# Hybrid attention and retention layer: the last block of the projections in another order, its weights' room handed on group by group

## The chip, the cores and the metric

The kernel runs on one core of a Trainium2 chip. The metric is the device time of one execution in microseconds (us), and less is better. "Before" and "after" are the kernel without and with the change.

## What is computed

```python
h = rms_norm(x, norm_gain)                       # x: 4096 tokens x 1024
qa, ka, va, ga, qr, kr, vr, gr = split(h @ w_in)
attn = dilated_attention(rope(qa), rope(ka), va) # 8 heads x 64, three (window, dilation) branches
ret  = retention(rotate(qr), rotate(kr), vr)     # 4 heads, key 64, value 128, chunks of 128 tokens
ret  = group_norm(ret) * ret_gn_gain
out  = rms_norm(x + concat(silu(ga) * attn, silu(gr) * ret) @ w_out, final_gain)
```

All of it is float32. A float32 operand is held as a rounded part (hi) and a rest (lo), and a product is three matmuls (`mm3`, lines 49 to 51 of the profile): hi by hi, hi by lo, lo by hi.

## The kernel before

There are three phases. **Phase 1** projects blocks of 512 tokens (`BLK`, 8 blocks) onto q, k, the retention's q and k together (group r), and the attention's values v. A block has six half groups, `GROUPS`: q0, q1, k0, k1, r0, r1, each of two product tiles of 24 matmuls, and then four value tiles of 24 matmuls each. `rotate` (VectorE, lines 227 to 232, with ScalarE's `hl` for q and k at line 244) applies the positions' tables (`tabA` for q and k, `tabR` for r) and stores the result to device memory (`dr_q`, `dr_k`, `dr_r`) from SyncE's queue. It is called for a group when the next group's products have been issued. `store_values` (lines 257 to 266) scales a value tile on ScalarE into one of two tiles `vo` and issues six DMAs `dr_v<-vo` from ScalarE's queue: two of 256 KB, four of 64 KB.

**Phase 2** is the attention, head by head, from `dr_k` (a tile `kk` of 128 x 4096 for two heads) and `dr_q` (tiles q00 and q10 for the first half of the tokens, q01 and q11 for the second). S is the scores' matmul (line 615), P the exponentials on ScalarE. TensorE's gaps are filled with the retention by chunks of 128 tokens: V (the chunk's values, 24 matmuls of `w2` by `hc`), Rs (its scores) and so on, from a generator `filler`. Its order is set by a table of costs in nanoseconds: `LEAD` worth of it goes ahead of the first S, then a slot's worth behind each step of the attention. `hr` is a chunk of the transposed x (512 KB), `hc` its hi and lo halves (ScalarE line 404, GpSimdE line 405), `vch` the V tile copied out by ScalarE (line 984). **Phase 3** computes the gates and the output projection.

Every engine's order is fixed: the code is written in the order in which each engine issues it, and SyncE's and ScalarE's queues issue their DMAs in that order.

On the change of phase: the weights of q, k and r lie in a stack of pools. Behind the last block's groups (q, k, r) that stack is closed as a whole (`right.close(3)`, line 338), and the room goes to q, w2, the chunk tiles and kk. Everything of phase 2 is then loaded on SyncE's queue in the order `hr` (chunk 0), `w2` (8 DMAs of 256 KB), `kk` (4 of 512 KB), q00 and q10 (4 of 256 KB each), `hr` (chunk 1); `w2` is split into hi and lo, the last rotate is called, and the last block's four value tiles follow.

Each DMA of SyncE's and ScalarE's queues raises one of eight semaphores (DMAHW0 to DMAHW7), which are handed out in turn over both queues; a DMA that gets a semaphore waits at its issue until the DMA that had it before has landed, whichever queue that was on. A wait at the head of a queue holds everything behind it.

Of the kernel before, what the change touches and what calls it, by code (L numbers as in the profile page):

```python
# [8 lines left out]
F32 = mybir.dt.float32  # L9
# [8 lines left out]
LEAD = 1500.0  # L18
# [35 lines left out]
class Split:  # L54
# [3 lines left out]
    def __init__(self, nc, pool, name, src, ks=range(KT), scale=None):  # L58
        self.nc, self.pool, self.name, self.scale = nc, pool, name, scale
        self.src = [src[k * 128 : (k + 1) * 128, :] for k in ks]  # L60
        self.n, self.width = len(ks), src.shape[1]
        self.hi = pool.tile([128, self.n, self.width], F32R, name=f"{name}hi")
        self.raw, self.lo = {}, {}

    def slot(self, j, dtype):
        return self.pool.tile([128, self.width], dtype, tag=f"{self.name}{j}", name=f"{self.name}{j}")
# [6 lines left out]
    def split(self, j, lo_engine=None):  # L73
        hi, raw = self.hi[:, j, :], self.raw.pop(j)
# [12 lines left out]
    def at(self, j, cols):  # L87
        return self.hi[:, j, cols], self.lo[j][:, cols]
# [23 lines left out]
def phase1(tc, io, dr, right, ahead):  # L112
# [5 lines left out]
    with ExitStack() as ctx:  # L118
# [19 lines left out]
        W = {}  # L138
        for g in ("r", "k", "q", "v"):
            p = wp if g == "v" else right.open(f"p1w{g}")  # L140
            i = "qkrv".index(g)
            W[g] = Split(nc, p, f"w1{g}", io["w1"][:, i * 512 : (i + 1) * 512], scale=qgain if g == "q" else gain)
# [154 lines left out]

        GROUPS = [("q", 0), ("q", 1), ("k", 0), ("k", 1), ("r", 0), ("r", 1)]
        for b in range(NBLK):
            last = b + 1 == NBLK  # L300
            if b:
                tabA = load_tables(b, "A")
            xts, hnext, waiting = [], [], []
            for gi, (g, half) in enumerate(GROUPS):
# [8 lines left out]
                if gi == (0 if b else 2):  # L313
                    rb = along_free(b, diag)
                    scaled(tabA, rb)
                    if b:
                        tabR = load_tables(b, "R")
                        scaled(tabR, rb)
                waiting.append((g, half, ps))

                while len(waiting) > 1 and rb is not None:
                    w, x, (A, B) = waiting.pop(0)
                    rotate(b, w, x, A, B, tabR if w == "r" else tabA)
# [7 lines left out]
                if not last and gi >= 3:  # L331
                    while len(xts) < (2, 3, 4)[gi - 3]:
                        xts.append(load_xt(b + 1, len(xts)))
                    if gi == 4:
                        hnext.append(make_h(b + 1, 0, xts[0]))
            if last:
                right.close(3)
                qp = right.open("p2q")
                w2 = Split(nc, right.open("p2w2"), "w2", io["w2"], scale=gain)
                hcp = right.open("p2h")  # L340
                kka = right.open("p2ka")
                raw = load_x_chunk(nc, hcp, io, 0)
                ahead.update(w2=w2, qp=qp, hcp=hcp, kka=kka, hch={0: [split_h_chunk(nc, hcp, raw, 0, i) for i in range(2)]})
# [1040 lines left out]
```

## Time and profile before

| what | us |
|---|---|
| device time, median of three runs (2444.05, 2447.39, 2448.32) | 2447.39 |
| the profiled execution: its own time | 2448.65 |
| the profiled execution: span of the page | 2446.9 |
| TensorE matmul busy | 2343.5 (96%) |
| VectorE, ScalarE, GpSimdE busy | 1485.2, 989.6, 714.3 |

The page cuts the span into 40 slices of 61.2 us; its PE line is the busy share of TensorE in tenths, its PEclk line the clock that TensorE was granted, in tenths of full speed. The timeline lists instructions of one engine with their start and duration, and in brackets how long the engine had stood idle and what released it. The chain of waits is followed back from the last instruction to what released each step. A matmul's row is longer than the distance to the next, since they are pipelined: the distance of starts is what it costs.

### The profile page before, as it was taken

The numbers are of one execution on the slowest core, as the hardware profiler recorded it, in microseconds if no ns is written. First come the engines' busy times: TensorE is split into PE (matmuls) and PEld (weight loads), VectorE is DVE, ScalarE is ACT, GpSimd is POOL, SyncE is SP. The second block draws the span as 40 slices with busy tenths as digits, with TensorE's granted clock in tenths as the row PEclk, the third lists the DMA queues.
The fourth block names the chain that finished last, engine by engine and source line by source line (L and its number), as shares of the span: only waits on it lengthen the run. The fifth ranks groups of instructions, "written<-read, shape, count | busy, mean of one in ns | idle before, by whom it ended". The sixth has DMA issues, their size and how long they took to land.

```text
span 2446.9 us, 41800 instructions
## 1 busy us (share of the span) xinstructions
PE 2343.5 (96%) x14568; PEld 1985.9 (81%) x14568; DVE 1485.2 (61%) x3921; ACT 989.6 (40%) x2868; POOL 714.3 (29%) x761
## 2 busy tenths in 40 slices
PE   7999999999995999999999999996899999999998
PEld 5778888888884888887888887885889889999997
DVE  5643443444342878787777879786665565565554
ACT  4322212212212666666666666666222232232221
POOL 5312112112102535343444435354312112121110
PEclk9999999999997999999999999998999999999999
DMA  6343344343348565758576665746675656676663
GB/s 189 129 148 120 124 139 132 113 137 129 120 146 208 138 163 137 178 130 190 132 165 153 154 158 127 169 118 197 149 162 153 146 158 154 150 156 165 141 158 91
DMA packets 404067, 362.59 MB, mean 148 GB/s; under 512 B 191784, under 2 KB 334760, under 8 KB 398736
## 3 DMA queue, kind: packets, MB, share of 16 engines
q1 hardware_dynamic: 389216, 332.91, 52.5%
q10 hardware_dynamic: 14112, 25.43, 3.3%
q8 instruction: 115, 1.88, 0.3%
q0 software_dynamic: 528, 1.58, 0.2%
q14 instruction: 96, 0.79, 0.1%
HBM read 241.18 MB, written 118.64 MB: 147 GB/s over the span
## 4 chain that ended last, share of the span: by engine, by line
PE 74%; DMA 10%; DVE 5%; issue 2%; ACT 2%; POOL 2%; SPq 1%; ACTq 0%; POOLq 0%; DVEq 0%
PE S L615 8%; PE mm L49 8%; PE mm L50 8%; PE mm L51 8%; PE O L685 6%; PE T L652 5%; PE po L49 3%; PE po L50 3%; PE po L51 3%; PE g L50 3%; PE g L49 3%; PE g L51 3%; PE V L49 3%; DMA wb<-dr_w 2%; PE V L51 2%; PE V L50 2%
## 5 line engine op out<-in xcount | busy, mean ns | idle before, releaser
L636 DVE CUSTOM_DVE_ANT_0 S<-S,mask 128x256 f32<-128x256 f32 (+1 forms) x768 | 308.5, 402 | 168.7 <-PE S L615 139.1
L643 ACT ACTIVATE P<-S,nm 128x256 f32<-128x256 f32 (+1 forms) x768 | 337.4, 449 | 74.4 <-DVE nm L636 51.2
L51 PE MATMUL g<-h,wg 128*128 128x256 f32 x1024 | 290.6, 284 | 0.0
L652 PE MATMUL T<-ident,P 128*128 128x128 f32 x1368 | 213.3, 273 | 0.4 <-ACT P L643 0.4
L615 PE MATMUL S<-kk,qc 128*128 128x256 f32 x1024 | 186.5, 306 | 17.1 <-ACT P L643 11.8
L50 PE MATMUL po<-wo,m 128*128 128x512 f32 x512 | 201.7, 394 | 0.0
L51 PEld LDWEIGHTS g<-h,wg 128*128 128x128 f32 x1024 | 197.6, 193 | 0.1
L685 PE MATMUL O<-pt,v 128*64 128x128 f32 (+1 forms) x1968 | 196.0, 325 | 0.2 <-ACT pt L662 0.2
L615 PEld LDWEIGHTS S<-kk,qc 128*128 128x128 f32 x1024 | 149.8, 190 | 45.5 <-issue 28.9
L41 ACT ACTIVATE m<-e 128x256 fp32r<-128x256 f32 x128 | 53.3, 417 | 323.9 <-DVE e L1123 171.7
L405 POOL TENSOR_TENSOR hc<-hr,hc 128x512 fp32r<-128x512 f32 x64 | 85.9, 1343 | 319.3 <-ACT hc L404 249.4
L49 PE MATMUL po<-wohi,m 128*128 128x512 f32 x448 | 175.7, 392 | 2.1 <-DVE x L1170 2.1
L1177 POOL TENSOR_TENSOR rs<-v,mhalf 128x1 f32<-128x1 f32 x32 | 17.3, 541 | 549.2 <-DVE v L1175 549.2
L51 PE MATMUL po<-wohi,m 128*128 128x512 f32 x448 | 176.4, 394 | 0.0
L159 POOL TENSOR_TENSOR sq<-sq,sq 128x512 f32<-128x512 f32 x56 | 76.2, 1361 | 326.8 <-ACT sq L155 326.8
L685 PEld LDWEIGHTS O<-pt,v 128*64 128x64 f32 x1968 | 121.4, 136 | 60.7 <-issue 31.0
L652 PEld LDWEIGHTS T<-ident,P 128*128 128x128 f32 x1368 | 163.7, 141 | 1.1 <-ACT P L643 1.1
L49 PE MATMUL g<-h,wg1hi 128*128 128x256 f32 x512 | 146.5, 287 | 14.2 <-ACT h L439 14.2
L643 ACT ACTIVATION_READ_ACCUMULATOR P<-S,nm 128x1 f32 x768 | 158.0, 206 | 0.0
L50 PE MATMUL g<-h,wg1hi 128*128 128x256 f32 x512 | 148.9, 291 | 2.2 <-DVE h L440 1.7
L49 PE MATMUL g<-h,wg0hi 128*128 128x256 f32 x512 | 145.0, 283 | 4.7 <-ACT e L1116 4.7
L50 PE MATMUL g<-h,wg0hi 128*128 128x256 f32 x512 | 144.8, 283 | 0.0
(207 smaller groups left out, 6097.9 us busy)
## 6 DMA issues: line engine op xcount, KB each, us to landing
hr<-in_xT_dram SPq DMA_DIRECT2D x64, 512.0 KB
q<-dr_q SPq DMA_DIRECT2D x128, 256.0 KB
wb<-dr_w SPq DMA_DIRECT2D x128, 192.0 KB
o<-dr_o SPq DMA_DIRECT2D x192, 128.0 KB
v<-dr_v SPq DMA_DIRECT2D x94, 256.0 KB
xt<-in_xT_dram SPq DMA_DIRECT2D x64, 256.0 KB
dr_q<-hl SPq DMA_DIRECT2D x32, 512.0 KB
dr_k<-hl SPq DMA_DIRECT2D x32, 512.0 KB
```

Source lines behind the costliest of these rows:

```text
L41: nc.scalar.activation(dst[:, 0], src, AF.Copy)
L49: nc.tensor.matmul(out, wh, xh, start=first and i == 0, stop=False)
L50: nc.tensor.matmul(out, wh, xl, start=False, stop=False)
L51: nc.tensor.matmul(out, wl, xh, start=False, stop=last and i == n - 1)
L159: nc.gpsimd.tensor_tensor(sums[b], sums[b], sq, ALU.add)
L405: nc.gpsimd.tensor_tensor(hc[:, :, 1, :], src, hc[:, :, 0, :].bitcast(F32), ALU.subtract)
L615: nc.tensor.matmul(s[:, j * 256 : (j + 1) * 256], qq[h, t, half][:, off : off + 128] if br == 0 else it["q"][:, t, i, :], rhs, start=(j == ...
L636: nc.vector.tensor_tensor_reduce(sv, sv, mask[:, it["br"], c0:256], 1.0, BIG, ALU.add, ALU.min, accum_out=nm[:, col : col + 1])
L643: nc.scalar.activation(it["P", i // 2][:, i % 2, c0:256], sv, AF.Exp, bias=nm[:, col : col + 1], scale=-1.0, accum_out=den[:, col : col + 1])
L652: nc.tensor.transpose(t[:, j * 128 : (j + 1) * 128], it["P", bank][:, j // 2, j % 2 * 128 : j % 2 * 128 + 128], ident)
L685: nc.tensor.matmul(o[64 * bank : 64 * bank + 64, c0 : c0 + 128 * m], vt[h, br, idx // 8][:, idx % 8, :], it["pt"][:, a : a + m, :].rearran ...
L1177: nc.gpsimd.tensor_tensor(rs, v, mhalf, ALU.pow)
```

## The change

The last block runs its groups as `LASTG`: r0, r1, q0, q1, k0, k1, and loads the table of r first. `Split.hi` becomes tiles of at most four k-steps. The stack of pools is laid out so that each group's room is wanted by one successor: the hi tiles of r lie in the room of q00 and q10, the weights of q share pool, tags and slots with `w2`. `make_room` issues the load of q00 and q10 when r's products have been issued, and w2's when q's have. After the groups, `hr` of chunk 0 and the first 3584 columns of `kk` (4 DMAs of 448 KB) go ahead of the last rotate, which is now k1's, the last 512 columns (4 DMAs of 64 KB) behind it. w2 is split behind the load of chunk 1. And `LEAD` is 8000 in place of 1500. The name `qp` becomes a pair of pools, one for each half of the tokens.

```diff
-LEAD = 1500.0
+LEAD = 8000.0
...
+        qp = ahead["qp"] = {0: right.open("p2q")}
+        wpool = ahead["wpool"] = right.open("p12w")
         for g in ("r", "k", "q", "v"):
-            p = wp if g == "v" else right.open(f"p1w{g}")
+            p = {"v": wp, "q": wpool}.get(g) or right.open(f"p1w{g}")
...
+                tag="w" if g == "q" else None,
+                room=[(qp[0], "q00"), (qp[0], "q10")] if g == "r" else None,
...
+        def make_room(gi):
+
+            if gi == 1:
+                ahead["qq"] = {(0, i, 0): load_q(nc, qp, dr, 0, i, 0) for i in range(2)}
+            if gi == 3:
+                ahead["w2"] = Split(nc, wpool, "w2", io["w2"], scale=gain, tag="w")
+                ahead["w2"].load(xp.tile([128, BLK], F32, tag="x", name="raw1"))
+
         GROUPS = [("q", 0), ("q", 1), ("k", 0), ("k", 1), ("r", 0), ("r", 1)]
+
+        LASTG = [("r", 0), ("r", 1), ("q", 0), ("q", 1), ("k", 0), ("k", 1)]
...
-            for gi, (g, half) in enumerate(GROUPS):
+            for gi, (g, half) in enumerate(LASTG if last else GROUPS):
...
+                if last:
+                    make_room(gi)
             if last:
-                right.close(3)
-                qp = right.open("p2q")
-                w2 = Split(nc, right.open("p2w2"), "w2", io["w2"], scale=gain)
-                hcp = right.open("p2h")
-                kka = right.open("p2ka")
+                right.close(2)
+                qp[1] = right.open("p2q1")
+                hcp, kka = ahead["hcp"], ahead["kka"] = right.open("p2h"), right.open("p2ka")
                 raw = load_x_chunk(nc, hcp, io, 0)
-                ahead.update(w2=w2, qp=qp, hcp=hcp, kka=kka, hch={0: [split_h_chunk(nc, hcp, raw, 0, i) for i in range(2)]})
-                w2.load(xp.tile([128, BLK], F32, tag="x", name="raw1"))
-                ahead["kk"] = load_k(nc, kka, dr, 0)
+                kk = load_k(nc, kka, dr, 0, cols=slice(0, S - BLK))
+                w, x, (A, B) = waiting.pop(0)
+                rotate(b, w, x, A, B, tabs["A"])
+                ahead["kk"] = load_k(nc, kka, dr, 0, cols=slice(S - BLK, S), t=kk)
+                ahead["hch"] = {0: [split_h_chunk(nc, hcp, raw, 0, i) for i in range(2)]}
+                ahead["hr"] = load_x_chunk(nc, hcp, io, 1)
                 for k in range(KT):
-                    w2.split(k)
-                ahead["qq"] = {(0, i, 0): load_q(nc, qp, dr, 0, i, 0) for i in range(2)}
-                ahead["hr"] = load_x_chunk(nc, hcp, io, 1)
-                w, x, (A, B) = waiting.pop(0)
-                rotate(b, w, x, A, B, tabR)
+                    ahead["w2"].split(k)
```

**SyncE's queue at the end of phase 1.** In brackets stands what a row waits for at its issue. Before, from chunk 0's load on:

```order
L396 DMA hr_5089<-in_xT_dram 128x8x128 [waits DMAHW7_49,PE_49]
...
L71 DMA raw_5097<-in_w_dram 128x512 [waits DMAHW7_49]
L415 DMA kk_5113<-dr_k 32x4096 [waits DMAHW0_49]
L415 DMA kk_5113<-dr_k 32x4096 [waits DMAHW3_49] x3
L486 DMA q_00_5142<-dr_q 32x2048 [waits DMAHW3_49,PE_49]
L486 DMA q_00_5142<-dr_q 32x2048 [waits DMAHW5_49]
...
L486 DMA q_10_5147<-dr_q 32x2048 [waits DMAHW3_49]
L396 DMA hr_5152<-in_xT_dram 128x8x128 [waits DMAHW4_49,Pool_49]
```

Now (q00, q10 and w2 stand further up, between the stores of the groups):

```order
L421 DMA hr_5113<-in_xT_dram 128x8x128 [waits DMAHW7_49,PE_49]
L440 DMA kk_5115<-dr_k 32x3584 [waits DMAHW0_49,PE_49]
L440 DMA kk_5115<-dr_k 32x3584 [waits DMAHW1_49]
L440 DMA kk_5115<-dr_k 32x3584 [waits DMAHW6_49]
L440 DMA kk_5115<-dr_k 32x3584 [waits DMAHW5_49]
L260 DMA dr_k<-hl_5130 128x2x512 [waits DMAHW4_49,DVE_49]
L260 DMA dr_k<-hl_5134 128x2x512 [waits DMAHW7_49,DVE_49]
L440 DMA kk_5115<-dr_k 32x512 [waits DMAHW1_49]
L440 DMA kk_5115<-dr_k 32x512 [waits DMAHW3_49]
L440 DMA kk_5115<-dr_k 32x512 [waits DMAHW5_49]
L440 DMA kk_5115<-dr_k 32x512 [waits DMAHW7_49]
L421 DMA hr_5148<-in_xT_dram 128x8x128 [waits DMAHW1_49,Pool_49]
```

Eight loads of w2 and eight of q have left the stretch between chunk 0 and chunk 1; k1's two stores and four small loads of kk have come into it, and chunk 1 is still the last of it.

**ScalarE's queue, third value tile's store and what follows the fourth.** Now:

```order
L271 ACTIVATE vo_5265<-mm_5240,rs_all 128x512 [waits DMAHW5_49,DMAHW0_49,PE_49]
L273 DMA dr_v<-vo_5265 8x16x512 [waits Activation_49]
L276 DMA dr_v<-vo_5265 8x16x512 [waits DMAHW1_49]
L280 DMA dr_v<-vo_5265 8x4x512 [waits DMAHW2_49]
L280 DMA dr_v<-vo_5265 8x4x512 [waits DMAHW3_49]
L280 DMA dr_v<-vo_5265 8x4x512 [waits DMAHW5_49]
L280 DMA dr_v<-vo_5265 8x4x512 [waits DMAHW6_49]
...
L429 ACTIVATE hc_5442<-hr_5148 128x4x128 [waits DMAHW1_49]
L1009 ACTIVATE vch_5451<-V_5423,rs_all 128x512 [waits PE_49]
L429 ACTIVATE hc_5457<-hr_5148 128x4x128 [waits Pool_49]
L429 ACTIVATE hc_5509<-hr_5477 128x4x128 [waits DMAHW4_49,Pool_49]
L668 ACTIVATE P_5486,den_5483<-S_5487,nm_5482 128x128 [waits DVE_49,PE_49]
```

Before, two P of the first scores stood ahead of chunk 1's first `hc`; now three `hc` and a `vch` stand ahead of the first P. The waits on DMAHW5 in the two listings are on each other: the fourth `kk` of 3584 columns on the first value tile's fourth DMA, the third value tile's fifth DMA on that `kk`, the third `kk` of 512 columns on that DMA.

**TensorE at the start of phase 2.** Before, behind the three k-steps of chunk 0 that `LEAD` called for:

```order
L50 MATMUL V_5415<-w_5124,hc_5091 128x512
L51 MATMUL V_5415<-w2hi,hc_5091 128x512
L615 MATMUL S_5430<-kk_5113,q_00_5142 128x256
L615 MATMUL S_5430<-kk_5113,q_10_5147 128x256
L615 MATMUL S_5430<-kk_5113,q_00_5142 128x256
```

Now, behind all eight k-steps of chunk 0 (V_5423):

```order
L51 MATMUL V_5423<-w2hi,hc_5145 128x512
L49 MATMUL V_5453<-w2hi,hc_5442 128x512
...
L51 MATMUL V_5453<-w2hi,hc_5442 128x512
L896 MATMUL Rs_5463<-qbd_5398,rkh_5415 128x256
...
L896 MATMUL Rs_5463<-qbd_5398,rkl_5416 128x256
L49 MATMUL V_5453<-w2hi,hc_5442 128x512
...
L51 MATMUL V_5453<-w2hi,hc_5442 128x512
L640 MATMUL S_5487<-kk_5115,q_00_4808 128x256
```

The first S has gone behind 24 matmuls of chunk 0, two k-steps of chunk 1, the six Rs and two more k-steps of chunk 1: 42 matmuls in place of 9.

## Rows read from the trace of the kernel before

**Rows 1.** The page's slices of the span: busy tenths of TensorE and granted clock in tenths, 40 slices.

```profile
PE   7999999999995999999999999996899999999998
...
PEclk9999999999997999999999999998999999999999
```

**Rows 2.** Windows around the change of phase: busy us and count of TensorE matmul, weight load, VectorE, ScalarE, GpSimdE, then granted clock, DMA share and GB/s.

```profile
700.00:720.00 20.00, 20.00 (x88) 16.22 (x87) 10.47 (x14) 4.55 (x4) 0.00 (x0) 1.00 0.28 105
720.00:740.00 20.00, 20.00 (x88) 16.35 (x88) 6.61 (x9) 4.45 (x7) 3.00 (x2) 1.00 0.71 190
740.00:750.00 10.00, 10.00 (x46) 8.29 (x45) 6.35 (x10) 3.02 (x5) 0.20 (x1) 1.00 0.48 105
750.00:760.00 10.00, 5.21 (x23) 3.96 (x22) 1.69 (x6) 1.10 (x2) 5.67 (x9) 0.93 0.78 229
760.00:770.00 10.00, 0.00 (x0) 0.00 (x0) 0.87 (x3) 0.69 (x1) 3.00 (x4) 0.50 0.76 242
780.00:790.00 10.00, 6.33 (x20) 5.36 (x21) 1.43 (x7) 1.43 (x5) 1.27 (x1) 0.53 1.07 245
790.00:800.00 10.00, 10.00 (x69) 8.48 (x68) 7.03 (x23) 7.09 (x24) 5.19 (x5) 1.00 0.90 159
```

**Rows 3.** Timeline of TensorE: first product of the last group, first value matmul, first and last V ahead of the scores, the first scores and the V behind them.

```profile
708.90 0.39 PE L49 MATMUL mm<-h,w1rhi 128*128 128x512 f32 x1
...
731.22 0.39 PE L49 MATMUL mm<-w1vhi,h 128*128 128x512 f32 x1
...
753.00 0.39 PE L49 MATMUL V<-w2hi,hc 128*128 128x512 f32 x1
...
754.82 0.39 PE L51 MATMUL V<-w2hi,hc 128*128 128x512 f32 x1
778.42 0.55 PE L615 MATMUL S<-kk,q 128*128 128x256 f32 x1 [23.21 <-DMA q<-dr_q]
783.67 0.98 PE L615 MATMUL S<-kk,q 128*128 128x256 f32 x3 [4.70 <-DMA q<-dr_q]
...
788.29 1.05 PE L615 MATMUL S<-kk,q 128*128 128x256 f32 x4
...
789.69 0.39 PE L51 MATMUL V<-w2hi,hc 128*128 128x512 f32 x1
...
790.60 0.64 PE L615 MATMUL S<-kk,q 128*128 128x256 f32 x4
791.07 0.49 PE L652 MATMUL T<-ident,P 128*128 128x128 f32 x3
```

**Rows 4.** The chain of waits through the change of phase: start, us, what.

```profile
723.47 10.16 DMA hr<-in_xT_dram
...
745.76 7.95 DMA dr_v<-vo
...
757.66 12.37 DMA dr_v<-vo
...
771.32 4.30 DMA dr_v<-vo
775.98 7.56 DMA q<-dr_q
```

**Rows 5.** SyncE's queue, 733 to 790: who waited for what, us in total, times, longest.

```profile
SPq L415 <- DMA kk<-dr_k: 16.5, 2, 9.0
SPq L486 <- DMA dr_v<-vo: 10.8, 4, 8.4
```

**Rows 6.** Timeline of ScalarE and its queue: `hl` of a k group, the w2 halves, the store of the first value tile, the `hc` and `vch` of phase 2.

```profile
711.07 2.29 ACT L244 ACTIVATE hl<-o 128x512 fp32r<-128x512 f32 x2 [8.46 <-DVE o L231]
...
733.72 1.15 ACT L404 ACTIVATE hc<-hr 128x512 fp32r<-128x512 f32 x2 [20.36 <-DMA hr<-in_xT_dram]
734.78 2.79 ACT L80 ACTIVATE w2hi<-w,gain_all 128x512 fp32r<-128x512 f32 x4
...
744.43 0.67 ACT L257 ACTIVATE vo<-mm,rs_all 128x512 f32<-128x512 f32 x1
745.13 0.60 ACTq L259 DMA_DIRECT2D dr_v<-vo  x1
...
786.58 0.62 ACT L404 ACTIVATE hc<-hr 128x512 fp32r<-128x512 f32 x1
790.80 0.69 ACT L984 ACTIVATE vch<-V,rs_all 128x512 f32<-128x512 f32 x1 [3.60 <-PE V L51]
```

**Rows 7.** Timeline of GpSimdE: the load of the retention's k for chunk 0, the last step of its preparation for Rs, a lo half of `hc`.

```profile
757.55 0.72 POOL L845 DMA_DIRECT2D rk<-dr_r  x1
...
766.53 1.51 POOL L859 TENSOR_TENSOR qbd<-rq,qbd 64x256 fp32r<-64x256 f32 x2
787.33 1.27 POOL L405 TENSOR_TENSOR hc<-hr,hc 128x512 fp32r<-128x512 f32 x1 [19.29 <-ACT hc L404]
```

**Rows 8.** The chain of waits elsewhere: a store of 64 KB and loads of `hr` of phase 3 (512 KB).

```profile
1239.31 3.16 DMA dr_o<-os
...
1919.90 4.99 DMA hr<-in_xT_dram
...
2100.98 7.31 DMA hr<-in_xT_dram
```

More of the change, by code (lines that the diff above doesn't have):

```diff
@@ L138, in phase1 @@
         W = {}
+        qp = ahead["qp"] = {0: right.open("p2q")}
+        wpool = ahead["wpool"] = right.open("p12w")
         for g in ("r", "k", "q", "v"):
[L140 removed]
+            p = {"v": wp, "q": wpool}.get(g) or right.open(f"p1w{g}")
             i = "qkrv".index(g)
[L142 removed]
+            W[g] = Split(
+                nc,
+                p,
+                f"w1{g}",
+                io["w1"][:, i * 512 : (i + 1) * 512],
+                scale=qgain if g == "q" else gain,
+                tag="w" if g == "q" else None,
+                room=[(qp[0], "q00"), (qp[0], "q10")] if g == "r" else None,
+            )
         def load_xt(b, k):
@@ L322, in phase1 @@
                     w, x, (A, B) = waiting.pop(0)
-                    rotate(b, w, x, A, B, tabR if w == "r" else tabA)
+                    rotate(b, w, x, A, B, tabs["R" if w == "r" else "A"])
                 if b == 0 and gi == 1:
@@ L406, in split_h_chunk, with load_k @@
     return hc
-def load_k(nc, pool, dr, h, dma=None):
+def load_k(nc, pool, dr, h, dma=None, cols=slice(0, S), t=None):
     dma = dma or nc.sync.dma_start
-    t = pool.tile([128, S], F32R, tag="kk", name="kk2")
+    t = t or pool.tile([128, S], F32R, tag="kk", name="kk2")
     for i in range(2):
@@ L423, in load_x_block @@
 def load_x_block(nc, pool, io, b, dma=None):
-    t = pool.tile([128, KT, TB], F32, tag="q00", name="hr3")
+    t = pool[0].tile([128, KT, TB], F32, tag="q00", name="hr3")
     for i in range(2):
@@ L432, in split_h @@
 def split_h(nc, pool, raw, i, gain, rb):
-    t = pool.tile([128, KT // 2, 2, TB], F32R, tag=("q10", "q01")[i], name="h3")
+    t = pool[i].tile([128, KT // 2, 2, TB], F32R, tag=("q10", "q01")[i], name="h3")
     for k in range(KT // 2):
@@ L481, in load_q @@
     dma = dma or nc.sync.dma_start
-    t = pool.tile([128, S // 2], F32R, tag=f"q{i}{half}", name=f"q2_{i}{half}")
+    t = pool[half].tile([128, S // 2], F32R, tag=f"q{i}{half}", name=f"q2_{i}{half}")
     for dup in range(2):
@@ L1262, in early3 @@
             wg = ahead["wg"] = [
-                Split(nc, p, f"wg{i}", io["w3"][:, i * 512 : (i + 1) * 512])
+                Split(nc, (ahead["wpool"], p)[i], f"wg{i}", io["w3"][:, i * 512 : (i + 1) * 512], tag=("w", None)[i])
                 for i in range(2)
```

33 lines of the change are left out of this document (19 added, 14 removed).

## The prediction

> **What bounds the kernel now.** I read the page's slices first. TensorE is at nine tenths or more nearly everywhere; two slices fall out, the thirteenth (734 to 795 us) at 5 tenths and the twenty-eighth, at the change to phase 3, at 6 [rows 1]. The change touches the first. The windows cut it finer: full until 750, 5.21 us of ten busy in 750 to 760, nothing in 760 to 770, 6.33 at a granted clock of 0.53 in 780 to 790, full at 1.00 from 790 [rows 2]. So nothing else has to be looked at: whatever the change gives or costs it gives or costs here. The timeline names the hole: after nine V matmuls TensorE stands 23.21 us for q, issues one S, stands 4.70 us again for q, and then runs slowly [rows 3]. The slow part is the half level of the clock (0.50 to 0.53 of 2.4 GHz, that is 1.2 GHz), to which it fell while the engine stood. Its price from the rows: from 783.67 to 789.69 stand seven S and eleven V; at the distances of the full level (V 0.23, from 753.00 to 754.82 eight times; four S 0.47, from 790.60 to 791.07) that is 0.8 + 2.5 = 3.3 us in place of 6.0, so 2.7, and I take 2.6 for the part behind the second wait. **The loss before is 23.2 + 4.7 + 2.6 = 30.5 us.**
>
> Why q is late is in the chain: chunk 0's `hr` 10.16 us, w2, then stores of values (7.95, 12.37 and 4.30 us), then q 7.56 [rows 4]. A store of values from ScalarE's queue holds a load on SyncE's queue: SyncE waited 10.8 us on `dr_v<-vo`, and 16.5 us, 9.0 at most, on `kk` loads one behind the other [rows 5]. These are the shared completion semaphores, and they outlive the change.
>
> **What goes.** A pair of groups takes 22.3 us (708.90 to 731.22 [rows 3]), so r's products, now first, end near 686.6 and q's near 708.9. Behind these come the loads of q00 and q10 and of w2; with a rotate, a store and 15 us of transfer they have landed long before 753. The 23.2 and 4.7 us on q are gone. The order of the groups itself costs TensorE nothing: the same 24-matmul tiles, busy 20.00 of 20 in 700 to 720 and in 720 to 740 [rows 2], and a group's rotate is hidden under the next group's 11 us. The seven PSUM tiles, two to a group, let TensorE run on for about another group when a slow store of r holds a rotate. Were that cover gone, the excess over it would be paid, of a store that takes up to 12.37 [rows 4]: 0 to 1.4 us, taken as 0.
>
> **What comes in its place.** `LEAD` now asks for 42 matmuls ahead of the first S. Chunk 0's 24 V take 24 x 0.23 = 5.5 us, so they run from 753.0 to 758.5. The next matmul needs chunk 1's `hc`, hence `hr` of chunk 1, which is last on SyncE's queue. When it lands (call it T) decides everything. Step by step, on the clock of before, in which the last group ends at 731.22 in both:
>
> 1. The last rotate is now k1's. Its `hl` ends 4.46 us behind the products (708.90 to 711.07 + 2.29 [rows 3, 6]): 735.7. ScalarE then does two `hc` (1.15) and eight w2 halves at 0.70 (2.79 for four) [rows 6]: 742.5. The first `vo` ends at 743.2; before it began at 744.43, so about a microsecond sooner. Its six DMAs leave 0.63 apart (745.13, 745.76 [rows 4, 6]), the fourth at 745.2.
> 2. The first three large `kk` loads leave when k1's products end, the fourth waits for that fourth store: 745.2 + 0.6 + 4.3 (the quickest store in the chain, [rows 4]) = 750.1. A `kk` load took 8.2 us in the mean when serialised (16.5 over 2) and 9.0 at most [rows 5]; with 448 of 512 KB I take 8.2: landed at 758.3.
> 3. The third value tile's fifth DMA waits for that `kk`: 758.3 + 0.6 + 4.3 = 763.2. The third small `kk` waits for it, the fourth and chunk 1 stand behind it on the queue: chunk 1 leaves at about 764.2. The first small `kk`, on whose landing chunk 1 also waits, is a 64 KB transfer; one such store took 3.16 us [rows 8]. It leaves when the third value tile's second store lands, near 758, so it is back by 761 and does not decide.
> 4. `hr` of 512 KB took 10.16 us beside the w2 loads and 4.99 to 7.31 in phase 3 [rows 4, 8]. The queues are emptier here than at 723: I take 7.3. T = 771.5, in round numbers **T = 771**, bounds 766 (both the `kk` and the `hr` as quick as the quickest 512 KB here, 4.99) to 777 (9.0, 10.16 and a store 2 us slower).
> 5. Behind T come `hc` on ScalarE, 0.62, and its lo half on GpSimdE, 1.27 [rows 6, 7]: TensorE starts at T + 1.9. `vch` (0.69) runs beside it. The Rs that follow need the retention's k: its last preparation ended at 766.53 + 1.51 = 768.0 [rows 7], hidden.
>
> The idle time is then 772.9 - 758.5 = 14.4 us, and the clock will have fallen again as it did before; the same 2.6 us follow. **Loss after 17.0; gain 30.5 - 17.0 = 13.5 us.** Profiled, 2448.65 - 13.5 = 2435.1; the median of the runs stands 1.3 below that execution, so I say **2434.0**. Per microsecond of T the time moves by one: T = 766 gives 2429, T = 777 gives 2440.
>
> **Small edits, costed at nothing.** `Split.hi` in tiles of four k-steps frees room sooner, at w2 to gates too; the waits there are on other transfers and keep their place. The slot of each attention step shrinks by 6500 / 376 = 17 ns, which only spreads the filler; a full TensorE does not mind. Four more DMAs shift all later semaphores by some places; a shift costs or saves at most about one short store, 3.16 us [rows 8], which I keep as a width of 2. The second half of q is issued behind the chunk loads and should land some 10 us before it is read, if not, that is the rival "second wait" below.
>
> **Rivals.**
>
> *Nearly the whole hole closes.* If `hr` of chunk 1 lands before 758 TensorE goes on to two k-steps of chunk 1 (1.4 us, to 760) and then meets Rs, whose preparation ended at 768.0 before. So the hole does not vanish: 8 us, up to 3 less if its load, issued at 757.55, is quicker than it was, and 2.6 for the clock: loss 7.6 to 10.6, time 2424.5 to 2427.5. Against it: chunk 1 stands behind eight `kk` loads, and those behind stores that begin at 743. Chance 0.14.
>
> *A second wait.* As forecast, and chunk 2's `hr` (waiting for chunk 1's lo half on GpSimdE, so T + 3.3, landing about T + 10.6) or the second half of q is late too. The work between is V of chunk 1 and its scores, some 8 us; a wait of 3 to 8 us follows: 2437 to 2442. Chance 0.10.
>
> *The four small loads of kk run one behind the other.* From 758 four times 3.16 us [rows 8] is 12.6, so chunk 1 leaves at 770.6 in place of 764.2, and the time is 2440.4. Against it: three of the four wait for different transfers and can overlap. The Trainium skill leans this way, and against cutting a load in pieces altogether: its page "DMA: Bandwidth & Descriptors", section "Anatomy of one DMA — SWDGE (gpsimd) path", puts about 2 us of fixed cost on each transfer. By that, an estimate, four more in series put 8 us on T and make it 2442; the row of 3.16 us for 64 KB agrees with a large fixed part, but no run so far shows whether such parts add up or overlap here. Chance 0.04.
>
> *Slower: the stores and the loads of kk hold each other at their longest rows.* The ring of step 2 and 3 has no slack, and each of its links may be as slow as before. With the store at 12.37 the fourth `kk` leaves at 758.2, lands 9.0 later at 767.2, the fifth store is back at 780.2, `hr` leaves at 781 and lands at 791.2 (10.16). TensorE then stands from 758.5 to 793.1: loss 37.2, time 2454. It decides from T = 784.5 (idle 27.9 as before), and is measurable from 789.4. For it: one value tile's store did take 12.37, with the DMA engines moving 229 to 242 GB/s [rows 2, 4]. Against it: that was while w2, kk and q came in together; w2 and q have left. Chance 0.06.
>
> *It does not do what it says:* q's early load blocked on the queue by r's store, say, and the hole staying as it is, 2447. The room of q00 is freed by r's last product and the order of the queue shows nothing between but stores that were there before. Chance 0.06.
>
> **How the numbers follow.** Forecast (T 766 to 777, 2429 to 2440) 0.60, the rivals in their order 0.14, 0.10, 0.04, 0.06, 0.06. A measurement of this kernel tells about 0.2%, 4.9 us, from no change. Faster by more than that, below 2442.5: the forecast, the first rival and most of the two behind it, 0.86. Slower, above 2452.3: the ring of stores and `kk` loads, and a little of what I have not seen, 0.07. Within: 0.07. The range of 8 in 10 takes in the forecast and the first three rivals: 2422 (the first rival, with the 2 us of shifted semaphores) to 2443.
>
> **What would show it.** In the profile after: no S waiting for q; SyncE's q loads before 710; in the slice of 734 to 795 a single hole of TensorE beginning near 758.5, ended by the `hc` of chunk 1, some 14 us long, then a clock of about 0.5 for a few us; 42 matmuls ahead of the first S. SyncE waiting on `dr_v<-vo` at the loads of `kk`, and ScalarE waiting for `kk` within the third value tile's store. Wrong would be a hole that begins earlier (values or chunk 0 late), one that is ended by Rs or `kk`, a stall of TensorE between 662 and 753, or a second hole within 20 us behind the first.

## The result, and the profile after

The changed kernel takes **2427.38 us** (median of 4 runs, 2425.27 to 2429.18) against 2447.86 us of the kernel before on the same chip: ratio 0.9916, interval 0.9897 to 0.9934, a gain of 20.5 us. Forecast were 2434.0 us, a gain of 13.5. The direction and the new wait are as forecast, but the gain is half as large again, and it is not made where the forecast put it: at the change of phase 6.5 us were won in place of 13.5, and some 15 us in the attention behind it, which the forecast had left out.

The profiled execution took 2426.76 us, its span is 2425.0, 21.9 less than before. The page's slices, busy tenths and granted clock, show the old slice of 5 now at 6, its clock at 8 in place of 7, and at this scale nothing else:

```profile
PE   7999999999996999999999999996899999999998
PEclk9999999999998999999999999998999999999999
```

The windows around the change of phase (the columns as in [rows 2]) show the hole later and shorter than before, but longer than the 14.4 us forecast:

```profile
760.00:770.00 10.00, 1.86 (x9) 1.20 (x7) 0.87 (x3) 1.37 (x2) 4.03 (x7) 0.85 0.88 267
770.00:780.00 10.00, 0.00 (x0) 0.00 (x0) 0.00 (x0) 0.00 (x0) 1.36 (x2) 0.50 0.63 230
780.00:790.00 10.00, 5.77 (x25) 4.80 (x25) 0.69 (x1) 1.72 (x3) 3.92 (x4) 0.62 0.40 116
```

TensorE's timeline, against [rows 3]: the first V, the last V of chunk 0, the first V of chunk 1 with the idle time before it, the first V behind the six Rs, and the first S. There is one hole, and no S waits for q any more:

```profile
756.25 0.39 PE L49 MATMUL V<-w2hi,hc 128*128 128x512 f32 x1
...
761.47 0.39 PE L51 MATMUL V<-w2hi,hc 128*128 128x512 f32 x1
784.23 0.80 PE L49 MATMUL V<-w2hi,hc 128*128 128x512 f32 x1 [22.37 <-ACT vch L1009]
...
787.94 0.39 PE L49 MATMUL V<-w2hi,hc 128*128 128x512 f32 x1
...
789.32 0.64 PE L640 MATMUL S<-kk,q 128*128 128x256 f32 x4
```

From 784.23 to 787.94 lie six V and six Rs, at a granted clock of 0.62 in that window (0.50, the level of 1.2 GHz, in the one before). At the distances of the full level that is 6 x 0.23 + 0.71 (six Rs in the chain at 802.36) = 2.1 us in place of 3.7, so 1.6 us more. Loss after: 22.4 + 1.6 = 24.0; before it was 30.5.

The chain of waits through the change of phase (start, us, what), against [rows 4], is where to look for what made the hole:

```profile
734.99 7.94 DMA hr<-in_xT_dram
...
751.63 4.21 DMA dr_v<-vo
755.86 6.52 DMA kk<-dr_k
762.41 0.69 ACT vo L271
...
764.39 9.65 DMA dr_v<-vo
774.06 4.81 DMA dr_v<-vo
778.89 4.08 DMA dr_v<-vo
...
802.36 0.71 PE Rs L896 x6
```

The first link is that of the prediction's step 2: a store of values, then the fourth `kk` on its semaphore. At the end stand three stores one behind the other. The link between, from that `kk` to the third value tile, is inferred by the profile, and ScalarE's queue below does not bear it out.

SyncE's queue between 733 and 790 (who waited for what, us in total, times, longest), against [rows 5], and its timeline:

```profile
SPq L440 <- DMA dr_v<-vo: 23.8, 4, 17.2
SPq L260 <- DMA dr_v<-vo: 11.1, 2, 9.9
```

```profile
692.78 9.31 SPq L511 DMA_DIRECT2D q<-dr_q  x8
...
735.54 20.62 SPq L440 DMA_DIRECT2D kk<-dr_k  x4
766.12 2.06 SPq L260 DMA_DIRECT2D dr_k<-hl  x2
773.41 3.01 SPq L440 DMA_DIRECT2D kk<-dr_k  x4
777.75 0.39 SPq L421 DMA_DIRECT2D hr<-in_xT_dram  x1
```

The loads of q have left the stretch (692.78). But four issues of `kk` took 20.62 us; k1's two stores, next on the queue, waited 11.1 us for stores of the second value tile and left from 766.12; and the first small `kk` left only at 773.41, when the third value tile's second store (256 KB, issued at 763.76) had landed, 9.65 us behind its issue. `hr` of chunk 1 leaves at 777.75. ScalarE's timeline, against [rows 6], shows these stores, value tile by value tile:

```profile
748.98 0.67 ACT L271 ACTIVATE vo<-mm,rs_all 128x512 f32<-128x512 f32 x1
...
756.32 5.97 ACTq L280 DMA_DIRECT2D dr_v<-vo  x4
762.41 0.69 ACT L271 ACTIVATE vo<-mm,rs_all 128x512 f32<-128x512 f32 x1 [7.39 <-DMA kk<-dr_k]
...
763.76 0.59 ACTq L276 DMA_DIRECT2D dr_v<-vo  x1
...
767.84 0.69 ACT L271 ACTIVATE vo<-mm,rs_all 128x512 f32<-128x512 f32 x1 [4.75 <-DMA dr_v<-vo]
...
774.69 4.78 ACTq L280 DMA_DIRECT2D dr_v<-vo  x4
782.97 0.63 ACT L429 ACTIVATE hc<-hr 128x512 fp32r<-128x512 f32 x1 [14.45 <-DMA dr_v<-vo]
783.51 0.67 ACT L1009 ACTIVATE vch<-V,rs_all 128x512 f32<-128x512 f32 x1
```

The profile does not count the issuing of a DMA as busy time. Of the 7.39 us that it puts down to `kk`, ScalarE spent all but about 0.3 issuing the second tile's stores, the last four of them from 756.32 to 762.29; the third `vo` began 0.12 us behind, as it does in a run below that has no `kk` on these semaphores (761.11, 761.23). So that ScalarE waited for the `kk` is not shown: the hold that this trace shows goes one way, from the stores to SyncE's loads, and the stores are late through ScalarE's own issuing and through earlier stores. ScalarE had issued the last of them at 779.47 (774.69 + 4.78); then it stood for chunk 1's `hr` (the profile names a store that landed at the same time), and `hc`, `vch` and the first V of chunk 1 followed one behind the other.

**Where the rest comes from.** Windows of the kernel before: the first block's end, and 800 us of the attention:

```profile
100.00:160.00 60.00, 58.02 (x251) 45.99 (x250) 24.84 (x33) 12.11 (x20) 14.04 (x11) 1.00 0.39 130
800.00:1600.00 800.00, 782.74 (x6121) 655.42 (x6120) 634.96 (x2308) 533.92 (x1844) 353.63 (x403) 1.00 0.64 153
```

The same windows after:

```profile
100.00:160.00 60.00, 57.84 (x230) 45.22 (x229) 25.03 (x34) 11.50 (x19) 13.99 (x11) 0.91 0.39 131
800.00:1600.00 800.00, 796.08 (x6275) 668.49 (x6272) 644.13 (x2369) 549.66 (x1897) 366.42 (x412) 1.00 0.64 156
```

In the attention TensorE is idle for 13.3 us less (796.08 - 782.74), which no term of the forecast held. What it and VectorE waited for there, 800 to 1640 (us in total, times, longest). Before, TensorE, then VectorE:

```profile
PE S L615 <- ACT P L643: 13.5, 15, 2.4
```

```profile
DVE qc L591 <- DMA dr_o<-os: 5.4, 2, 2.9
...
DVE qc L591 <- DMA q<-dr_q: 4.9, 3, 3.0
DVE qc L591 <- DMA raw<-dr_st: 4.7, 1, 4.7
...
DVE qc L591 <- DMA rk<-dr_r: 3.6, 1, 3.6
```

After, TensorE, then VectorE:

```profile
PE S L640 <- ACT P L668: 1.1, 4, 0.3
```

```profile
DVE qc L616 <- DMA raw<-dr_st: 2.5, 2, 2.1
DVE qc L616 <- DMA q<-dr_q: 2.1, 3, 1.3
```

`qc` is the copy of the next head's q, made by VectorE between the softmax steps. While it waits for a transfer, the softmax stands behind it, P comes late, and S waits for P. The wait that TensorE shows (for ScalarE's P) is two steps away from what caused it. These waits fell from 18.6 us in four rows to 4.6 in two, and S's wait from 13.5 to 1.1.

The other windows go against the change: at the end of the first block the granted clock was 0.91 in place of 1.00, and the first V stands at 756.25 in place of 753.00, 3.3 us later (0.6 to 0.7 later in the four later profiles of the changed code with a clock of 1.00 there, so some 2.6 of it is the clock). The order of the work is the same in both there; the dip showed in eight of the twelve later profiles (0.89 to 0.97), in the kernel before with another lead among them, so it is not put down to the change. The sum, up to the last S waits of the attention (1661.17 before, 1642.14 after, 19.0 earlier): +3.3 up to the first V, -6.5 at the change of phase, -13.3 of idle time in the attention, and about -2 for a granted clock of 0.98 from 1500 to 1600 before, 1.00 after: -18.5. Another 2.9 of the 21.9 lie in phase 3 and weren't followed up.

### The profile page after: what moved, and what is told of

The parts are those of the page before. It is cut to its first block, busy times and chain, and to the rows that moved or that the text cites. A ratio compares the mean times of both kernels' runs of the same rounds, so it can differ in the third digit from the quotient of the medians.

```text
span 2425.0 us, 41805 instructions
## 1 busy us (share of the span) xinstructions
PE 2339.9 (96%) x14568; PEld 1984.7 (82%) x14568; DVE 1486.3 (61%) x3921; ACT 992.1 (41%) x2868; POOL 721.8 (30%) x761
## 4 chain that ended last, share of the span: by engine, by line
PE 81%; DMA 6%; DVE 4%; ACT 2%; issue 1%; POOL 1%; ACTq 1%; SPq 1%; POOLq 0%; DVEq 0%
PE S L640 9%; PE O L710 7%; PE mm L50 7%; PE mm L49 7%; PE mm L51 7%; PE T L677 6%; PE po L50 4%; PE po L51 4%; PE po L49 4%; PE g L50 4%; PE g L49 4%; PE g L51 4%; PE V L49 3%; PE V L51 2%; PE V L50 2%; DMA wb<-dr_w 1%
## 5 line engine op out<-in xcount | busy, mean ns | idle before, releaser
L1202 POOL TENSOR_TENSOR rs<-v,mhalf 128x1 f32<-128x1 f32 x32 | 17.3, 540 | 554.5 <-DVE v L1200 554.5
L49 PE MATMUL g<-h,wg0hi 128*128 128x256 f32 x512 | 145.0, 283 | 4.7 <-ACT e L1141 4.7
L1141 ACT ACTIVATE e<-g 128x256 f32<-128x256 f32 x128 | 48.3, 378 | 237.1 <-PE g L51 233.4
```

What stands on the lines that cost most here:

```text
L49: nc.tensor.matmul(out, wh, xh, start=first and i == 0, stop=False)
L1141: nc.scalar.activation(e, g, AF.Silu)
```

## The experiments

Two questions stood open. In the attention: does the lead itself remove the waits (theory L), or do four more DMAs, which move all later semaphores by four places (rival D)? And at the change of phase: which of the waits makes the hole? In the recorded expectations the stores and the `kk` loads hold each other, the "ring" of the prediction's steps 2 and 3.

### Change without its lead; lead without the change

The first run puts the old lead into the changed kernel:

```diff
-LEAD = 8000.0
+LEAD = 1500.0
```

> The changed kernel with LEAD back at 1500, all else as changed. Theory L (the lead ahead of the first S takes the later waits of phase 2 away, because the retention's loads, which stand in front of q's on SyncE's queue, are then no longer late): the 13 waits of S on P between 800 and 1640 come back, some 13 us of idle TensorE, and the q casts of VectorE wait some 20 us on DMAs again. At the change of phase TensorE issues 9 V, then stands for the last columns of kk, which landed at 779.6 in the changed kernel: a hole of about 22 us and 2 for the clock, where before lost 30.5. Time about 2441 us. Rival D (the four more DMAs of the diff shift every later semaphore, and that alone moved phase 2): the waits stay away, time 2427 to 2430.

Measured: 2436.02 us (2432.31 to 2442.08), ratio 0.9954, 0.9937 to 0.9972. TensorE's waits in the attention are back as they were:

```profile
PE S L640 <- ACT P L668: 13.0, 13, 2.2
```

The DMAs are the changed kernel's, the lead is the old one, and the waits follow the lead: D falls. The second run puts the new lead into the kernel before:

```diff
-LEAD = 1500.0
+LEAD = 8000.0
```

> The kernel before with LEAD 8000, nothing else of the change. Theory L: phase 2 loses its waits of S on P (13.5 us before, 1 to 3 now); at the change of phase chunk 1's load still leaves at about 776.5, behind q, so the hole moves from the q wait to the wait for chunk 1's hc: from 758.5 to about 786, 2 us of half clock behind it, no gain there. Time about 2434 us. Rival D: phase 2 keeps its waits, time 2446 to 2449.

Measured: 2432.99 us (2428.97 to 2437.3), 0.9937, 0.992 to 0.9954. S waits for P 1.3 us in all, with 42 matmuls ahead of the first S and a hole of 28.74 us at the change of phase, as long as before. So **one constant, without the new order, gives 14.9 us of the 20.5**; the new order without the constant gives 11.9. The two together give 6.3 us less than their sum (26.8). Of that 2.6 is seen in the hole: the new order takes 9.0 us of idle time from it with the lead at 1500 (27.9 to 18.9, which are waits of 6.44 us for `kk`, 9.70 for P and 2.75 for `vch`) and 6.4 with the lead at 8000 (28.74 to 22.37). The rest is not explained, and each ratio is only known to about 4 us either way.

### The stores of the last block on another queue

GpSimdE issues the last block's 24 value stores, which take none of the eight semaphores that SyncE and ScalarE share:

```diff
+            store = nc.gpsimd.dma_start if b + 1 == NBLK else nc.scalar.dma_start
-            nc.scalar.dma_start(dr["v"][0, n * 128 : (n + 1) * 128].rearrange("(r l) e -> l r e", r=16), vf)
+            store(dr["v"][0, n * 128 : (n + 1) * 128].rearrange("(r l) e -> l r e", r=16), vf)
...
```

> The changed kernel with the last block's value stores issued by GpSimdE, which has semaphores of its own. Theory S (kk, k1's stores and so chunk 1 are late because they wait on the value stores' semaphores): all kk has left by 746 and landed before 755, chunk 1 leaves at about 747 in place of 777.75 and lands by 757. TensorE goes on from 24 V to two k-steps of chunk 1 without a stop. The next wait is Rs on the retention's k, whose load now stands behind 24 more issues on GpSimdE: about 776 in place of 771.4. Hole 12 to 14 us in place of 22.4; time about 2418 us. Rival B (the transfers themselves are slow, 230 GB/s of traffic): kk's last piece still lands at about 780 and the time stays at 2425 to 2429.

Measured: 2423.08 us (2420.59 to 2423.7), 0.9895, 0.9877 to 0.9912. SyncE no longer waits for the stores: all `kk` are issued by 745.7, `hr` of chunk 1 leaves at 747.63 in place of 777.75. TensorE still loses 1.60 us, and then this:

```profile
776.47 0.80 PE L51 MATMUL V<-w2hi,hc 128*128 128x512 f32 x1 [14.82 <-POOL hc L431]
```

The lo half of chunk 1 stood on GpSimdE behind the 24 stores, five tables, four loads and the preparation of Rs, until 775.16. The wait has moved to the engine that now issues, and the time stays some 5 us above the expected.

### Chunk 1 alone past the ring

The prediction says that the landing of chunk 1's `hr` "decides everything". Here GpSimdE issues that load, and all else stays:

```diff
-                ahead["hr"] = load_x_chunk(nc, hcp, io, 1)
+                ahead["hr"] = load_x_chunk(nc, hcp, io, 1, nc.gpsimd.dma_start)
```

> The changed kernel with the load of chunk 1 (hr, 512 KB) issued by GpSimdE behind chunk 0's lo halves; the value stores stay. Theory S: it leaves at about 747 and lands by 756; TensorE goes on to chunk 1 at 761.7, stops 1.4 us later for Rs (the retention's k ready at 771.4), and stops again at about 774 for the last columns of kk, which still wait on the value stores, until about 780. Two holes, 8 and 6 us, in place of one of 22.4; time about 2419 us. Rival B: chunk 1 lands 10 us or more behind its issue and pushes kk out by as much, time 2425 to 2430.

Measured: 2425.86 us (2419.05 to 2431.18), 0.9909, 0.9889 to 0.9928, no different from the change itself. `hr` left at 746.89 and its hi half was made at 751.99, 31 us sooner than in the changed kernel. Yet the hole was 20.15 us, ended by `vch`. ScalarE's timeline tells why:

```profile
781.30 0.69 ACT L1009 ACTIVATE vch<-V,rs_all 128x512 f32<-128x512 f32 x1 [8.56 <-DMA dr_v<-vo]
```

`vch` of chunk 0 stands on ScalarE behind the fourth value tile's stores. Neither theory's hole came: theory S did not have `vch`, and rival B did not have a load that lands early. So two things had to be early, chunk 1 and ScalarE's own queue, and the value stores hold both. The prediction's "decides everything" was wrong.

### The ring cut without loading GpSimdE with the stores

The stores stay on ScalarE; all `kk`, k1's two stores and chunk 1's `hr` go to GpSimdE, so that the two queues no longer share semaphores in this stretch:

```diff
-                kk = load_k(nc, kka, dr, 0, cols=slice(0, S - BLK))
+                kk = load_k(nc, kka, dr, 0, nc.gpsimd.dma_start, cols=slice(0, S - BLK))
...
-                rotate(b, w, x, A, B, tabs["A"])
+                rotate(b, w, x, A, B, tabs["A"], nc.gpsimd.dma_start)
...
```

> The changed kernel with all kk loads, k1's two stores and chunk 1's load issued by GpSimdE, whose semaphores are its own; the value stores stay on ScalarE's queue. Theory S (the stores are held by kk and kk by the stores through shared semaphores): the four value stores go at their undisturbed distance of 5.3 us (749, 754, 760, 765), the fourth has left by 769, vch and chunk 1's hc follow it, GpSimdE's lo half comes behind the retention's preparation: TensorE goes on at 770 to 773 in place of 784.2, a hole of 9 to 11 us; time 2414 to 2417 us. Rival B (traffic): the last store leaves at 775 or later, hole 18 us or more, time 2423 to 2428.

Measured: 2431.07 us (2429.6 to 2435.33) with the kernel before at 2458.37 on that chip, 0.9896, 0.9875 to 0.9917. The hole:

```profile
775.40 0.79 PE L49 MATMUL V<-w2hi,hc 128*128 128x512 f32 x1 [14.54 <-ACT vch L1009]
```

14.5 in place of 22.4: with `kk`, k1's stores and chunk 1 off the shared semaphores about 8 us of the hole go. The time does not show them clearly: 0.9896 against the change's 0.9916, with intervals that overlap, and 2414 to 2417 were expected. What is left is the issuing of the stores on ScalarE: the four `vo` came 5.7, 5.9 and 8.2 us apart in place of 5.3, the last since the third tile's six stores were issued from 761.94 to 769.27 with hardly a gap, single ones in up to 2.18 us where 0.59 is usual. The fourth tile's were issued by 774.61, and `vch` began at 774.66. What stretches an issue no run here shows. More of the hole than expected belongs to the stores.

### All known holds taken away

As in the first run with stores on GpSimdE, and besides: chunk 1's lo half and chunk 0's preparation of Rs on VectorE, the first `rq`, `rk` and the tables loaded by SyncE.

```diff
-    nc.gpsimd.tensor_tensor(hc[:, :, 1, :], src, hc[:, :, 0, :].bitcast(F32), ALU.subtract)
+    lo = nc.vector if c == 1 else nc.gpsimd
+    lo.tensor_tensor(hc[:, :, 1, :], src, hc[:, :, 0, :].bitcast(F32), ALU.subtract)
...
-        first_rk = load_rk(0, nc.gpsimd.dma_start)
+        first_rk = load_rk(0)
...
```

> The run with the value stores on GpSimdE, and beyond it: chunk 1's lo halves and chunk 0's preparation for Rs by VectorE, and the loads of the retention's first k and q and of the tables of phase 2 by SyncE, so that nothing of the start of phase 2 but the first two v loads stands behind the value stores on GpSimdE. If the wait of 14.8 us there was GpSimdE's order alone, TensorE goes on from chunk 0 to chunk 1 with the stop of 1.6 us for vch and then waits for Rs until the retention's k, issued at about 757, has landed and been split: 764 to 768. Holes of 3 to 7 us in all; time 2411 to 2415 us. If it was traffic, the loads land at 770 or later and the time stays at 2419 or more.

Measured: 2416.3 us (2415.38 to 2422.32), 0.9837, 0.9813 to 0.9861:

```profile
764.88 0.79 PE L49 MATMUL V<-w2hi,hc 128*128 128x512 f32 x1 [5.57 <-ACT vch L1011]
```

The hole is within the 3 to 7 us expected. The time is 1.3 us above the 2411 to 2415, on a chip on which the kernel before takes 10.5 us more than in the runs that the expectation was made from. Since it beats both kernels, it was run once more beside the changed kernel, on one other chip.

> The changed kernel once more, beside the others of this group: about 0.992 of the kernel before; waits of S on P between 800 and 1640 at 1 to 3 us.

> The version without the holds at the change of phase, on the same chip as the changed kernel: 10 to 14 us less than the changed kernel (a hole of 5.6 us in place of 22.4, and some of the clock's fall), 0.986 to 0.988 of the kernel before.

Measured, with the kernel before at 2456.1: the changed kernel 2435.05 us (2429.32 to 2436.17), 0.991, 0.9892 to 0.9928, hole 21.89, S's waits for P 1.4; the version without holds 2416.59 (2414.99 to 2420.57), 0.9843, 0.9824 to 0.9863, holes 4.33 and 1.81. The 18.5 us between the two are more than the 15.8 of idle time between their holes, and more than the 10 to 14 expected; the rest was not traced.

### How the lead removes the waits

Is there a best lead that comes round again, because what matters is only where a step of the filler falls within a head (theory P)?

```diff
-LEAD = 8000.0
+LEAD = 10400.0
```

> The changed kernel with LEAD 10400: 8904, the table's cost of one chunk of retention, more than 1500. Theory P (the lead is a phase: two chunks fall to each half of a head, so the chunk's loads always stand at the same place beside q's loads at the half's end; LEAD decides where): 10400 puts them where 1500 did, the waits of S on P between 800 and 1640 come back at 12 to 14 us and VectorE's q casts wait 18 to 22 us on DMAs; the hole at the change of phase stays as with 8000. Time 2438 to 2441 us. Rival M (more work ahead is more slack): the waits stay at 1 to 3 us, time 2425 to 2429.

Measured: 2434.23 us (2428.68 to 2438.32) with the kernel before at 2458.37, 0.9901, 0.988 to 0.9922. S waited 5.6 us in all, neither P's 12 to 14 nor the 1 to 3 of rival M. As worded both fall. A likely reason, not tested, is that the lead also shrinks the slot, so that the filler drifts against the heads. A lead between the two:

```diff
-LEAD = 8000.0
+LEAD = 4500.0
```

> The changed kernel with LEAD 4500. Theory Q: the retention's loads come 3000 ns of the table earlier against the attention than with 1500, which puts hr ahead of the q loads of a head's end and rq, rk, which come two k-steps behind, still among them: S waits on P 4 to 9 us, between the 13 of LEAD 1500 and the 1.1 of LEAD 8000. At the change of phase S comes behind seven V: TensorE runs on with S, as with LEAD 1500. About 0.993 of the kernel before. If more lead simply is more slack the waits lie in between as well, so this run alone decides nothing; with the 5.6 us of LEAD 10400 it shows whether the waits follow the size of the lead.

Measured: 2443.97 us (2440.66 to 2449.95), 0.9955, 0.9939 to 0.9971; S waited 11.0, more than expected.

What in the filler hurts q? SyncE's timeline at a head's end, before and then after:

```profile
1120.72 0.99 SPq L548 DMA_DIRECT2D q<-dr_q  x2
1121.80 0.39 SPq L396 DMA_DIRECT2D hr<-in_xT_dram  x1
1122.24 1.37 SPq L548 DMA_DIRECT2D q<-dr_q  x2
```

```profile
1121.03 1.79 SPq L573 DMA_DIRECT2D q<-dr_q  x4
...
1133.35 0.40 SPq L421 DMA_DIRECT2D hr<-in_xT_dram  x1
```

Before, the 512 KB of the next chunk's `hr` leave among the last loads of q, and `qc` waited 3.61 us there; after, `hr` leaves 12 us behind q, and `qc` waited 0.19. There is a second way as well: `hc` stands ahead of P on ScalarE, and at this head's end before it waited 2.26 us for `hr` itself (at 1130.42), after which S waited 1.24 us for P. From 800 to 1640 `hc` waited 4.2 us for `hr` before, against 18.6 for `qc`. Theory Q put the delay down to SyncE's queue and the semaphores that `hr` takes on it, so GpSimdE was given the chunk loads and `rq`, `rk` of the attention, at the old lead:

```diff
-LEAD = 8000.0
+LEAD = 1500.0
...
-                        hraw[c + 1] = load_x_chunk(nc, hcp, io, c + 1)
+                        hraw[c + 1] = load_x_chunk(nc, hcp, io, c + 1, nc.gpsimd.dma_start)
...
-                        res[c].update(load_rk(c))
+                        res[c].update(load_rk(c, nc.gpsimd.dma_start))
```

> LEAD 1500, and the retention's loads of phase 2 (hr, rq, rk) issued by GpSimdE in place of SyncE. Theory Q (with LEAD 1500 these loads fall among the last loads of q and raw at the end of a head, on the same queue, and make qc late, which makes S wait on P): VectorE's qc casts wait 8 us or less on DMAs between 800 and 1640 (21.7 with LEAD 1500), S waits on P 5 us or less (13.0); 8 to 10 us faster than LEAD 1500 alone, about 0.991 to 0.992 of the kernel before. Rival W (it is the traffic or the phase of ScalarE's and VectorE's own work, not the queue): S keeps 10 us or more of waits on P, 0.995 of the kernel before. GpSimdE then has three more issues per chunk, which may hold its own qc casts.

Measured: 2450.18 us (2446.06 to 2452.81) with the kernel before at 2456.1, 0.9972, 0.996 to 0.9985:

```profile
PE S L640 <- ACT P L668: 15.1, 18, 2.4
```

```profile
DVE qc L616 <- DMA q<-dr_q: 17.9, 6, 4.1
```

```profile
ACT hc L429 <- DMA hr<-in_xT_dram: 13.0, 10, 2.7
```

No better (15.1 against 13.0): `qc` waits for q no less than with `hr` on SyncE (17.9 us against 11.3 in the first run with the old lead), and `hc` waits more for `hr` (13.0 against 4.6). So Q falls: it is not SyncE's queue or its semaphores. Left was the transfer itself (theory T: the 512 KB share the DMA engines with q's), or effects of the lead on which engine's work falls together (rival E). At the old lead, the 30 loads of `hr` in the attention are left out, and chunks 2 to 31 use chunk 1's x:

```diff
-LEAD = 8000.0
+LEAD = 1500.0
...
-                        hraw[c + 1] = load_x_chunk(nc, hcp, io, c + 1)
+                        hraw[c + 1] = ahead["hr"]
```

> LEAD 1500 with the 30 loads of hr in phase 2 left out: chunks 2 to 31 are computed from chunk 1's x, all other work is done. Theory T (with LEAD 1500 the 512 KB of a chunk's hr are transferred among the last q loads of a head and hold them up, on whichever queue they were issued): VectorE's qc casts wait 8 us or less on DMAs between 800 and 1640 (21.5 with LEAD 1500), S waits on P 5 us or less (13.0), about 0.991 to 0.992 of the kernel before (LEAD 1500 with the loads: 0.9954). Rival E (the phase of the retention's work on ScalarE, VectorE and TensorE against a head's end, not its transfers): the waits stay at 10 us or more, 0.994 to 0.996.

Measured: 2425.49 us (2423.87 to 2428.37), 0.9909, 0.9893 to 0.9925:

```profile
PE S L640 <- ACT P L668: 1.7, 5, 0.5
```

With the old lead and no `hr` the waits go from 13.0 to 1.7, and TensorE is busy 794.87 of the 800 us. Rival E falls. This run together with the one before it, in which `hr` was off SyncE's queue and semaphores, leaves the transfers of `hr`: T holds in that sense. The two runs do not part its two ways, q late for `qc` and `hr` itself late for `hc`; by the waits the first is the larger at the old lead (11.3 against 4.6). That a lead of 8000 sets `hr` and q apart is seen at the one head's end above and was not followed up at the others. Why 4500 gives 11.0 and 10400 5.6 follows from no rule found here; the drift was not worked out head by head.

## Why the prediction was right or wrong, step by step

**What goes: right.** No S waits for q; its loads leave at 692.78, and w2's at 718.68. TensorE shows no stall between 662 and 761. The order of the groups cost nothing that can be seen.

**What comes in its place: right in kind, 8.0 us too short.** The hole, forecast from 758.5 to 772.9, lies from 761.86 to 784.23. Of the 11.3 us by which its end is later, 3.3 lie ahead of the first V (most of them the clock at the end of the first block) and move the start as well. Step by step:

- Step 1: the first `vo` was put at 742.5 and began at 748.98. ("About a microsecond sooner" than before was a slip, an end set against a start: 742.5 is 1.9 before 744.43.) Of the 6.5 us, 3.3 are those; the most of the rest is chunk 0's: `hr` landed at 742.9, and ScalarE waited 3.3 us for it with `hc`, w2 and `vo` behind, a wait which the step left out.
- Step 2: the fourth `kk` was put at 750.1 and left at 755.86, landing after 6.52 us in place of 8.2: at this point 4.1 us late, 0.8 more than the 3.3.
- Step 3, which failed: "The third value tile's fifth DMA waits for that `kk`: 758.3 + 0.6 + 4.3 = 763.2." That wait is not seen: the `kk` had landed at 762.38, before the tile's first store, and the fifth DMA left at 765.65, at the usual distance behind the fourth. What held chunk 1 is what the step set aside: the first small `kk` "leaves when the third value tile's second store lands, near 758, so it is back by 761 and does not decide". That store was issued at 763.76, ScalarE having taken 5.97 us over four of the second tile's where the prediction has 0.63 each, and took 9.65 us to land. The step's 4.3 is the row of a 64 KB store; this one has 256 KB, and its own row before was 12.37 [rows 4]. k1's two stores, which stand ahead of the small loads and waited 11.1 us, are not in the step at all. The small loads left from 773.41, chunk 1 at 777.75 in place of 764.2.
- Step 4: `hr` took 5.2 us at most in place of 7.3 (issued 777.75, `hc` at 782.97; the trace puts the end of that wait down to a store that landed at the same time). T is 783 or little less, outside the bounds 766 to 777. "When it lands (call it T) decides everything" fell with the run in which GpSimdE loads chunk 1: ScalarE's queue, busy with the stores, set nearly the same end.
- Step 5: right in size, 1.3 us from `hc` to the first V in place of 1.9, but not in kind: `vch`, which "runs beside it", is what the first V of chunk 1 waited for, and in the run with chunk 1 early it ended the hole some 29 us behind `hc`. The clock's price was 1.6 in place of 2.6, since Rs and V, not S waiting a second time, stood there.

The slower rival took the ring at its longest rows (12.37, 9.0) and put T at 791.2; the measured T lies between that and the forecast. It was right that the stores could be that slow, 12.37 being nearer to the 9.65 than 4.3 is, but the `kk` had no part in it. With `kk`, k1's stores and chunk 1 on GpSimdE 8 us of the hole go, and with every known hold gone 17.

**"Small edits, costed at nothing": wrong, and the largest error.** "The slot of each attention step shrinks by 6500 / 376 = 17 ns, which only spreads the filler; a full TensorE does not mind." TensorE was not full: 17.3 us of idle time lay in 800 to 1600 before, in pieces of 2.4 us at most, too small for a slice of 61 us to show. "So nothing else has to be looked at" was read from the slices and the windows around the hole alone (and three more slices, the first, the twenty-ninth and the last, are below nine tenths); the waits of the attention in one view would have shown 13.5 us of S on P. The lead took these waits away, and TensorE's idle time there fell by 13.3 us.

**The rivals.** Nearly the whole hole closing would have given 2424.5 to 2427.5, and the measured 2427.4 lies there by chance: the hole did not close. A second wait behind the first did not come. The small loads of `kk` did not run one behind the other: all four left within 3.01 us from 773.41, and chunk 1 stood 1.3 us for one of them. The Trainium skill, "DMA: Bandwidth & Descriptors", "Anatomy of one DMA — SWDGE (gpsimd) path", gives a fixed cost of about 2 us for a transfer that GpSimdE issues; the prediction's estimate, 8 us for four in series, took it over to loads of SyncE and added it up. Here they overlapped: the last was issued by 776.42 (773.41 + 3.01), and the first landed only about 777.7, when chunk 1, which waited for it, left. So the trace speaks against the adding up and says nothing against the fixed cost.

That 2434 was forecast and 2427.4 measured, and not further apart, is owed to two errors of opposite sign: 7.0 us too much gain at the hole, some 15 us too little in the attention.

## What to carry to other kernels

A slice of the page that reads nine tenths is not full: before costing a change of a planner's constant at nothing, list the waits of the stage it reorders, and follow the bounding engine's small waits (here S on P) through the engines to the transfer behind them. Where loads on one queue wait for stores on another, list for each load which transfer had its semaphore before, cost that transfer by the row of the same one (its size, its place), not by the quickest, and count the time that its queue needs to issue it; taking one load out moves the end only if nothing else stands behind the same stores. An idle time that the profile puts down to a DMA can be the engine's own issuing. And split a change with a constant in it: here the constant alone gave 14.9 us of 20.5, at one line.

## What the runs showed of the hardware

- A load on SyncE's queue waits at its issue for the store of ScalarE's queue that had its semaphore before, up to 17.2 us for one `kk`; with the `kk` loads, k1's stores and chunk 1 issued by GpSimdE the hole fell from 22.4 to 14.5 us.
- One issue of a DMA by ScalarE mostly took 0.59 us, but up to 1.84 us (after) and 2.18 us (with the `kk` on GpSimdE) among the last block's stores; no run shows why.
- The 512 KB loads of `hr` made the attention wait whichever queue issued them: S's waits for P were 13.0 us with `hr` on SyncE, 15.1 with it on GpSimdE, 1.7 without it; `qc`'s waits for q were 11.3 us and 17.9 in the first two.
- The granted clock from 100 to 160 us was 1.00 in some executions and 0.89 to 0.97 in others of nearly the same code; the first V of phase 2 came 1 to 4 us later with it, as much as some of the differences that one would like to read from a single profile.
